# A row-mean kernel: the last store is issued ahead of SyncE's waits for all other transfers

## Chip, cores, metric

One core of one Trainium2 chip. The metric is device microseconds of one launch, median over runs. Kernels that are compared ran in turns in one call on one chip; the three calls of the experiments were on chips 15, 11 and 15.

## Reference

```python
batch, seq, dim = 32, 512, 1024
x = np.random.randn(batch, seq, dim).astype(np.float32)     # 67.1 MB
return (np.sum(x, axis=-1) / divisor).astype(np.float32)    # divisor = 1024.0, 16384 means
```

## The kernel before

The input streams through a few large buffers by transfers that SyncE issues. VectorE sums most rows, ScalarE some. Results leave in three small stores: `res0` (8 KB), `res` (48 KB) and `fin` (8 KB). Only `fin` depends on the last load, `pb`. Engines and transfers report to each other by semaphores, on which the program adds, subtracts and waits (the code below); the landing of the last store shows in the trace as 16 steps of one, from 158.854 to 159.020 us. An event wait (EVENT_SEMAPHORE in the profile) is, in what follows, an instruction of SyncE that only waits: in this trace for one semaphore at 155.914, for two at 157.476. Its passage, below, is the time SyncE takes over it when the counts have long been reached; between two such waits in the changed kernel that is 53 to 64 ns from start to start.

```python
    load(pa, x_last[:, j, :c])
    load(pb[:, : D - c], x_last[:, j, c:])
    tc.keep_in_program_order(nc.sync.dma_start(out=o_first, in_=res0))
    tc.keep_in_program_order(nc.sync.dma_start(out=o_main, in_=res))
    dve_mean(pb[:, D - c : D - c + 1], pa, by=1.0)
    dve_mean(fin[:, j:], pb)
    tc.keep_in_program_order(nc.sync.dma_start(out=o_last, in_=fin))
```

The framework closes a program with a SyncE drain that waits for every transfer and every engine, then two barriers across the engines, with GpSimd clearing semaphores between them. In the trace the waits of SyncE, ScalarE, VectorE and TensorE for the first barrier lie between 158.272 and 158.335, GpSimd's clear (EVENT_SEMAPHORE_RANGE_CLEAR) takes 95 ns from 158.428, and their waits for the second lie between 158.751 and 158.813. This kernel had already been tuned there: a pass over the finished program moves the last store into that closing block, so that its 1.4 us of landing run beside the barriers, and puts the wait for the landing at the very end.

```python
def close_while_storing(nc, landed):
    body, end = nc.main_func.blocks[1], nc.main_func.blocks[-1]
    store = [i for i in body.instructions if i.engine == SP and ...][-1]
    drain = end.instructions[0]
    needs = {w.id: w for w in drain.sync_info.on_wait}
    ...                                   # the store's own transfer is taken off the list
    (done,) = [w for w in store.sync_info.on_wait if w.ant_name.startswith("DVE_")]
    del needs[done.id]                    # VectorE's last result: the store waits for it
    ...                                   # add, sub: +16 and -16 on the semaphore `landed`
    last = nc.sync.wait_ge(landed, 16).ins
    body.instructions = [i for i in body.instructions if i.name != store.name]
    end.instructions = [
        with_sync(drain, on_wait=tuple(needs.values())),        # five event waits and a drain
        with_sync(store, on_wait=(done,), on_update=(add,)),
        *end.instructions[1:-1],                                # the two barriers
        with_sync(last, on_update=(sub,)),                      # the wait for the landing
    ]
```

When the program is built, the drain's list becomes five event waits in front of a drain that keeps one wait; in the trace they start at 155.914 (one semaphore), 156.551, 157.146, 157.310 and 157.476 (two each), and the drain at 157.541.

## Time and profile before

| | before |
|---|---|
| time, median of 3 runs | 160.74 us (160.73 to 160.82) |
| span of the profiled execution | 159.1 us, 147 instructions |
| the DMA queue, share of 16 engines | 98.2% |
| VectorE, ScalarE busy | 117.2 us (74%), 18.5 us (12%) |

The span runs from the first to the last recorded instruction of the kernel; the time of the same execution, 160.59 us, is 1.5 us longer. From the list of transfers, these two rows (line's transfer, issuing queue, count, KB, us from issue to landing) are what SyncE's list waits for last:

```profile
out_dram<-res SPq DMA_DIRECT2D x1, 48.0 KB, 11.6
out_dram<-res SPq DMA_DIRECT2D x1, 8.0 KB, 33.6
```

They are small stores in the queue of the big loads: these 8 KB took 33.6 us to land, the 8 KB of `fin`, issued after the last load has landed, 1.4 us. The 8 KB store of `res0`, issued at 123.7 us, lands at 157.29; the 48 KB store of `res`, issued at 145.9, lands at 157.46: both just in front of VectorE's last result.

### The profile page before, as it was taken

What the parts mean: (1) busy time and instruction counts of PE and PEld (TensorE: products, weight loads), DVE (VectorE), ACT (ScalarE), POOL (GpSimd) and SP (SyncE); (2) the same over time, 40 slices, a digit from 0 to 9 for tenths busy, and PEclk for the clock granted to TensorE, in tenths of its full rate; (3) what the DMA queues carried; (4) which work ended last, traced back from release to release, by engine and by line L of the source; (5) the groups of instructions that cost most, each with busy time, mean ns of one, the idle gap of its engine ahead of it and who ended that gap; (6) DMA issues with size and microseconds to landing.
All of it is one profiled execution on the core that took longest, in us unless ns stands there. A gap on an engine that the chain in (4) does not pass through costs nothing.

```text
span 159.1 us, 147 instructions
## 1 busy us (share of the span) xinstructions
DVE 117.2 (74%) x29; ACT 18.5 (12%) x33; POOL 1.0 (1%) x7
## 2 busy tenths in 40 slices
DVE  0500059995999599977999599959995996395643
ACT  3000000000000000000000000000000900390684
POOL 0000000000000000000000000000000000001000
DMA  8999999979999999789999999699999999999894
GB/s 303 422 461 461 461 461 461 433 317 404 461 461 461 461 461 461 317 375 461 461 461 461 461 461 418 303 433 461 461 461 429 396 396 445 445 445 445 375 406 159
DMA packets 2448, 67.18 MB, mean 422 GB/s; under 512 B 656, under 2 KB 656, under 8 KB 912
## 3 DMA queue, kind: packets, MB, share of 16 engines
q1 hardware_dynamic: 2448, 67.18, 98.2%
HBM read 67.11 MB, written 0.07 MB: 422 GB/s over the span
## 4 chain that ended last, share of the span: by engine, by line
DMA 77%; DVE 21%; SPq 1%; issue 0%; DVEq 0%
DMA t<-in_x_dram 56%; DMA pb<-in_x_dram 21%; DVE res L177 20%; SPq L154 1%; DVE pb L164 0%; DVEq L231 0%
## 5 line engine op out<-in xcount | busy, mean ns | idle before, releaser
L177 DVE TENSOR_REDUCE res<-t 128x14 f32<-128x14336 f32 (+3 forms) x9 | 111.2, 12360 | 34.1 <-DMA t<-in_x_dram 34.1
L158 ACT ACTIVATE junk<-t 128x1024 f32<-128x1024 f32 x16 | 16.2, 1013 | 136.9 <-DMA t<-in_x_dram 136.9
L164 DVE CUSTOM_DVE_ANT_0 t<-t 128x512 f32<-128x512 f32 x8 | 5.1, 690 | 6.1 <-DMA t<-in_x_dram 6.1
L158 ACT ACTIVATION_READ_ACCUMULATOR junk<-t 128x1 f32 x16 | 3.0, 187 | 0.0
L179 POOL TENSOR_SCALAR res<-res 128x16 f32<-128x16 f32 (+1 forms) x2 | 0.7, 352 | 143.3 <-DVE res L177 143.3
L158 ACT ACT_TABLE_LOAD x1 | 1.3, 1283 | 1.7 <-PEq L217 1.7
L164 DVE DVE_READ_ACCUMULATOR2_ANT fin<- 128x1 f32 x9 | 0.8, 83 | 0.0
L164 DVE CUSTOM_DVE_ANT_0 pb<-pb 128x257 f32<-128x257 f32 x1 | 0.4, 428 | 0.2 <-DMA pb<-in_x_dram 0.2
L164 DVE CUSTOM_DVE_ANT_0 pa<-pa 128x256 f32<-128x256 f32 x1 | 0.4, 426 | 0.0
L151 POOL MEMSET pb<- 128x2 f32 x1 | 0.1, 99 | 1.3 <-POOLq L217 1.3
L217 POOL MEMSET const-bfloat16-1.0<- 128x1 bf16 x1 | 0.1, 102 | 0.0
L217 POOL MEMSET const-uint8-127<- 128x1 uint8 x1 | 0.1, 101 | 0.0
L217 POOL MEMSET const-float32-0.0<- 128x1 f32 x1 | 0.1, 98 | 0.2 <-issue 0.2
L217 POOL MEMSET const-float32-1.0<- 128x1 f32 x1 | 0.1, 98 | 0.0
L164 DVE DVE_READ_ACCUMULATOR2_ANT pb<- 128x1 f32 x1 | 0.1, 84 | 0.0
## 6 DMA issues: line engine op xcount, KB each, us to landing
t<-in_x_dram SPq DMA_DIRECT2D x7, 7168.0 KB, 35.6
t<-in_x_dram SPq DMA_DIRECT2D x1, 6144.0 KB, 33.3
t<-in_x_dram SPq DMA_DIRECT2D x1, 4608.0 KB, 27.2
t<-in_x_dram SPq DMA_DIRECT2D x2, 1024.0 KB, 19.2
t<-in_x_dram SPq DMA_DIRECT2D x1, 2048.0 KB, 31.7
pa<-in_x_dram SPq DMA_DIRECT2D x1, 256.0 KB, 33.9
pb<-in_x_dram SPq DMA_DIRECT2D x1, 256.0 KB, 33.9
out_dram<-res SPq DMA_DIRECT2D x1, 48.0 KB, 11.6
```

Of the source, the lines that this page charges most:

```text
L151: nc.gpsimd.memset(pb[:, D - c :], 0.0)
L154: tc.keep_in_program_order(nc.sync.dma_start(out=dst, in_=src))
L158: nc.scalar.activation(junk, src, COPY, scale=by, accum_out=dst)
L164: nc.vector.tensor_tensor_reduce(out=src[:, :h], in0=src[:, :h], in1=src[:, h:], scale=by, scalar=0.0, op0=ADD, op1=ADD, accum_out=dst,)
L177: nc.vector.reduce_sum(out=dst[:, j : j + d], in_=t[:, :d, :], axis=AX)
L179: nc.gpsimd.tensor_scalar_mul(out=dst, in0=dst, scalar1=scale)
L217: nc = _bacc.Bacc("TRN2", target_bir_lowering=False, num_devices=1)
```

## The change

The intent: SyncE should not have to get through its waits for all other transfers before it may issue the last store. Since the store needs only the results in `fin`, it goes first and takes along its own waits; the list comes behind it, still ahead of the barriers.

```diff
     end.instructions = [
+        with_sync(store, on_wait=store.sync_info.on_wait, on_update=(add,)),
         with_sync(drain, on_wait=tuple(needs.values())),
-        with_sync(store, on_wait=(done,), on_update=(add,)),
         *end.instructions[1:-1],
```

In the built program the store gets one event wait in front of it (a load and ScalarE's 16th result) and keeps its wait for VectorE; the five event waits and the drain stand behind it.

## The prediction

0.00 (step 1) + 0.00 (step 2) + 0.10 (step 5) = +0.10 us, hence 160.84 us; the +0.27 us of step 3 and the +0.05 us of step 4 are not added to it but go into step 5. That step took the steps of semaphore 2 for a chain from engine to engine, which was an assumption of mine.

> **What bounds the kernel now.** I read the page of the profiled execution first, then the chain of waits that ended last, then the last two microseconds by timeline and by line, then the time stamps of single instructions and semaphore updates in the trace, because everything the change touches lies in the last 1.5 us of 159.1 us.
>
> The page says what the body of the kernel is: one long load.
>
> ```profile
> DVE 117.2 (74%) x29; ACT 18.5 (12%) x33; POOL 1.0 (1%) x7
> q1 hardware_dynamic: 2448, 67.18, 98.2%
> ```
>
> The one DMA queue fills 98.2% of 16 engines' time with 67.18 MB; no engine is nearly as full. The change leaves all loads and all arithmetic alone, so some 157 of the 159.1 us cannot move. What remains is the end of the chain:
>
> ```profile
> 123.15 0.04 issue
> 123.19 33.94 DMA pb<-in_x_dram
> 157.13 0.02 issue
> 157.15 0.43 DVE pb L164
> 157.58 0.01 DVEq L231
> ```
>
> The last load (pb, issued at 123.19) lands at 157.13, and the last VectorE sum runs 157.15 to 157.58. The reader should note that no wait of SyncE stands between the load and that sum. The timeline shows what follows:
>
> ```profile
> 157.15 0.43 DVE L164 CUSTOM_DVE_ANT_0 pb<-pb 128x257 f32<-128x257 f32 x1 [0.16 <-DMA pb<-in_x_dram]
> 157.50 0.08 DVE L164 DVE_READ_ACCUMULATOR2_ANT fin<- 128x1 f32 x1
> 157.62 0.33 SPq L200 DMA_DIRECT2D out_dram<-fin  x1
> ```
>
> The store of fin starts 0.03 us after the accumulator read ends. The question of the whole case is what those 0.03 us are: the semaphore, or SyncE coming late out of its list of waits. SyncE's list of waits says who it waited for (total us, times, longest):
>
> ```profile
> SPq L231 <- DMA t<-in_x_dram: 9.7, 1, 9.7
> SPq L231 <- DMA pa<-in_x_dram: 0.6, 1, 0.6
> SPq L231 <- PEq L231: 0.6, 2, 0.4
> SPq L231 <- DMA pb<-in_x_dram: 0.6, 1, 0.6
> SPq L87 <- SPq L87: 0.3, 1, 0.3
> ```
>
> and the closing line L231, between 157.2 and 157.56 us, says when its instructions ran:
>
> ```profile
> L231 SPq EVENT_SEMAPHORE  x2: 28/28/28, 157.3 to 157.5; - x2
> L231 SPq DRAIN  x1: 7/7/7, 157.5 to 157.5; - x1
> ```
>
> The waits look large (9.7, 0.6, 0.6 us) but they are over before the store can go. By the stamps, SyncE's last two waits start at 157.310 and 157.476, its drain runs 157.541 to 157.548, VectorE's semaphore reaches its count at 157.598, and the store starts at 157.615. So SyncE was through its list 50 ns before the data existed. The 17 ns from semaphore to start are the same as at the earlier loads that waited for VectorE (121.286 to 121.302, 104.375 to 104.391: 16 ns each). The margin is thin, but the store is already as early as its data allows.
>
> The store's landing and the closing line then run beside each other:
>
> ```profile
> DMA to landing us min/median/max: 1.4/1.4/1.4
> ```
>
> Landing: the store's 16th increment is at 159.020, and the very last wait (the line L87 above, 0.3 us of waiting) ends at 159.053, which is the span. Closing: the store's issue ends at 157.947, SyncE's drain for the barrier runs 157.998 to 158.127, two barriers follow, and SyncE leaves the second at 158.768. The landing path thus beats the closing path by 159.036 - 158.768 = 0.27 us. That slack is what the change spends.
>
> [...] 0.33 us of issue, 1.4 us to landing. [...] a satisfied wait to the next instruction on SyncE, is 65 ns (157.476 to 157.541)[...]. [...] semaphore 2 steps nine times from 159.048 and nine times again from 160.362 to 160.720, which is 8 hops of 45 ns. I use it in step 5.
>
> **The change part by part.** I compared the two built programs. No load, no arithmetic and no other engine's order differ. On SyncE:
>
> 1. Moved: the store from behind five event waits and a drain to ahead of them. Its VectorE wait stays. Gain on the path: the store started 17 ns after its semaphore, so 0.00 us.
> 2. Added: one event wait ahead of the store (the last big load and ScalarE's 16th result). ScalarE's 16th step is at 157.079, the load's landing long before (137.688). It is through by about 157.1, 0.5 us before VectorE's 157.598. Cost 0.
> 3. Shifted: the five event waits and the drain now stand between the store's issue and SyncE's arrival at the first barrier. All they wait for has happened: the latest, the two earlier stores, landed at 157.293 and 157.459. So each costs only its passage. Start: 51 ns after the issue (157.947 to 157.998 now; 124.115 to 124.166 likewise for an event wait after a store). Then 6 x 65 ns = 0.39 us, so the barrier's drain starts at 158.388 in place of 157.998. Given back: that drain takes 129 ns directly behind the store (125 behind the first loads), but 7 ns where no DMA is just ahead; with 0.39 us in between I take 7. It ends at 158.395 in place of 158.127: closing is +0.27 us. Taking 54 ns (17 + 37, a one-semaphore wait and the smallest gap seen) or 89 ns (28 + 61, the gap between two waits on GpSimd) for 65 gives +0.20 to +0.41.
> 4. The end of the span: SyncE leaves the second barrier at 158.768 + 0.27 = 159.04; the store lands at 159.020 as before; the last wait follows 45 ns later (GpSimd's gap from drain to a satisfied wait) and ends near 159.10. Span +0.05 us. The slack has swallowed the rest.
> 5. Behind the span: [...] In the first series the steps are at 159.048, 159.082, 159.287, 159.331 and on; in the second the same steps are 34, 39, 44 ns apart. So the third step came late in the first series, by 205 - 39 ns. The first is 0.235 us after TensorE's sequencer leaves the kernel's last barrier (158.813), the third 0.234 us after SyncE ends (159.053); from that match I take the chain as TensorE first, SyncE third, SyncE late by its wait for the landing. With closing +0.27 the first two steps go to 159.318 and 159.352 and the third to 159.391, while SyncE's own end allows 159.334. The chain, and all that follows it, moves by 159.391 - 159.287 = +0.10 us: not the 0.27 of the closing path, not the 0.05 of the span. The order of the engines is inferred; no view names them.
>
> Sum: 0.00 + 0.00 + 0.10 = +0.10 us on 160.74: 160.84 us, or +0.06%.
>
> **Rivals.**
> (a) The intended gain: the store goes earlier and the end with it. For it: only 50 ns of margin, so in an execution where the two small stores land later than VectorE's last sum, SyncE would be late in the kernel before. Against: in the traced one the store went 17 ns after its semaphore; even removing all of the 28 ns after VectorE ends gives nothing like a per cent. It would make 160.65 to 160.74.
> (b) The closing path becomes the bound and costs in full: if the waits pass slowly[...]. Against: the 65 ns seen.
> (c) Full cover: the waits pass in 54 ns and the chain after the span hangs on the landing alone: 160.74 to 160.77.
> (d) Loads move: none. The store is 8 KB and goes after the last load has landed, so it can delay nothing.
>
> **Range and chances.** [...]the three runs of before spread over 0.09 us (160.73 to 160.82) and its profiled run took 160.59, so a run or a chip differs by as much as the effect. I put the middle at 160.84 and 8 in 10 at 160.6 to 161.1. 2% would be 3.2 us; nothing in the last 1.5 us can move that much, save a state I cannot see. Same 0.98, faster 0.01, slower 0.01.
>
> **What would show it.** In the changed profile the store's issue should again start about 17 ns after VectorE's last semaphore (step 1), with an event wait of SyncE near 157.1 ahead of it (2), five waits and a drain about 65 ns apart behind it, and a barrier drain of 7 ns (3); the wait for the landing should shrink from 0.3 us to under 0.1, and the span grow by 0.0 to 0.2 (4). I am wrong if the store starts earlier against its semaphore, if the barrier's drain still takes 0.13 us, [...]or if the time falls by more than the spread of the runs.

## The result and the profile after

The changed kernel took 161.01 us (median of 6 runs, 160.91 to 161.35), the kernel before 160.75 in the same rounds (160.63 to 160.82). The ratio is 1.002, interval 1.0007 to 1.0033. By the 2% mark that is the same; by the interval it is a small loss. A ratio here is the mean time of one kernel's fast runs over that of the other's of the same rounds, so it is not quite the ratio of the medians quoted.

The timeline of the last two microseconds, changed kernel (start, duration, engine, line):

```profile
157.36 0.43 DVE L165 CUSTOM_DVE_ANT_0 pb<-pb 128x257 f32<-128x257 f32 x1 [0.16 <-DMA pb<-in_x_dram]
157.71 0.08 DVE L165 DVE_READ_ACCUMULATOR2_ANT fin<- 128x1 f32 x1
157.82 0.33 SPq L201 DMA_DIRECT2D out_dram<-fin  x1
```

The store again follows the last accumulator read by 0.03 us: nothing was gained there. The whole group sits 0.2 us later than before because in this execution the last load landed at 157.33, not 157.13. So it is better to count from VectorE's last semaphore (157.598 before, 157.804 after) than from the start of the span.

SyncE's waits in the changed kernel (who waited, for whom, total us, times, longest):

```profile
SPq L201 <- ACT junk L159: 11.1, 1, 11.1
SPq L232 <- PEq L232: 0.6, 2, 0.4
SPq L201 <- DVE fin L165: 0.5, 1, 0.5
```

The waits at the closing line for the loads of t, pa and pb are gone from the list, and so is the last line of before, 0.3 us at line L87. That one was SyncE sitting at the end of the program until the store had landed. After the change the store has been down for 0.05 us when that last wait runs.

Where SyncE spent that time instead shows at the closing line between the store's issue and the first barrier. Before, from 157.95 to 158.15:

```profile
L231 SPq DRAIN  x1: 129/129/129, 158.0 to 158.0; - x1
```

After, from 158.15 to 158.59:

```profile
L232 SPq EVENT_SEMAPHORE  x5: 17/28/28, 158.2 to 158.4; - x5
L232 SPq DRAIN  x2: 7/7/7, 158.5 to 158.6; - x2
```

(Durations are ns: least, median, most; then first and last start.) One drain of 129 ns became five event waits, the drain of the list and the barrier's drain, now 7 ns. By the stamps the event waits start 53, 62, 64 and 61 ns apart, the list's drain 65 ns and the barrier's drain 59 ns later.

The remaining evidence is in single stamps, which no view lists; the table below gives them as us after VectorE's last semaphore. "Chain" is my name for the steps of semaphore 2 behind the kernel, which no instruction of the kernel touches. In before they are nine from 159.048 to 159.572 us and nine more from 160.362 to 160.720; between 159.475 and 160.138 the trace has a last update of 247 semaphores, numbers 7 to 255. The expectations call it the runtime's chain; whose it is, no trace shows. The time of an execution is the last step of that chain, counted from the start of the span, less 0.11 to 0.13 us in all fourteen traces: in before 160.72 and 160.59, in after 161.16 and 161.04, in the kernel tail30 below 161.38 and 161.26. So the last step stands for the metric.

| kernel | store starts | SyncE at the first barrier | TensorE ends | SyncE ends | chain: step 1 | step 2 | step 3 | step 5 | last step |
|---|---|---|---|---|---|---|---|---|---|
| before | 0.017 | 0.529 | 1.215 | 1.455 | 1.450 | 1.484 | 1.689 | 1.756 | 3.122 |
| after | 0.016 | 0.766 | 1.451 | 1.484 | 1.686 | 1.720 | 1.925 | 1.993 | 3.356 |
| difference | 0.00 | +0.24 | +0.24 | +0.03 | +0.24 | +0.24 | +0.24 | +0.24 | +0.23 |

SyncE's own end hardly moved, as predicted. The chain moved nevertheless, by all of the 0.24 us that SyncE lost on its way to the barrier.

### The profile page after: what moved, and what is told of

The parts are those of the page before. It is cut to its first block, busy times and chain, and to the rows that moved or that the text cites. A ratio compares the mean times of both kernels' runs of the same rounds, so it can differ in the third digit from the quotient of the medians.

```text
span 159.3 us, 148 instructions
## 1 busy us (share of the span) xinstructions
DVE 117.2 (74%) x29; ACT 18.5 (12%) x33; POOL 1.0 (1%) x7
## 4 chain that ended last, share of the span: by engine, by line
DMA 77%; DVE 21%; SPq 1%; issue 0%; DVEq 0%
DMA t<-in_x_dram 56%; DMA pb<-in_x_dram 21%; DVE res L178 20%; SPq L155 1%; DVE pb L165 0%; DVEq L232 0%
```

## The experiments

Theory A: what counts is when the kernel's two closing barriers are through; the chain starts from there, so each passage that stands between the store and SyncE's first barrier is paid in full. Theory B, which my prediction rested on: SyncE's wait for the landing holds the chain at its third step, so part of the loss is hidden. Theory C: the change also makes the loads end later, since the first trace had them 0.2 us later.

All kernels gave correct results. "Chain" is the last step after VectorE's last semaphore; before has 3.122 in its first trace and 3.129 in the second.

### Controls: the changed kernel twice more, the kernel before against itself

No edit (`after_again`, `after_last`, `before_again`).

> The changed kernel once more, unedited. Theory A (the whole closing path is paid: SyncE reaches its first barrier 0.24 us later against VectorE's last semaphore[...]): time +0.24 us over before, and the last load lands as in before, so the 0.2 us by which the loads ended later in its first trace were chance. Theory B (my prediction's step 5: SyncE's wait for the landing holds the runtime's chain at its third step, so part is hidden): +0.10 us. Theory C (the change also makes the last loads land 0.2 us later): +0.4 us and pb landing again near 157.33.

> The kernel before against itself: ratio 1.000, the interval shows what a run can tell (about 0.1% = 0.15 us). A and B: pb lands anywhere from 157.1 to 157.4 us; C: always near 157.13. In all: SyncE's barrier drain ends 0.53 us after VectorE's last semaphore, the third step of the runtime's chain 1.69 us after it.

> The changed kernel a third time, in the third place of its call: the +0.3 us of means so far is over the 0.24 us that the closing path shows in each trace. Theory A: the rest is when the loads end, which varies alike in both kernels: ratio 1.0015 (+0.24 us), trace again 0.24 us later from VectorE's last semaphore to the end. Theory C (loads made later by the change too): ratio 1.002 or more again with pb landing later than in the other traces of this call.

| run | median | ratio to before, 95% | pb lands | chain |
|---|---|---|---|---|
| after_again | 161.15 us, 6 runs | 1.0020 (1.0004 to 1.0036) | 157.152 | 3.360 |
| after_last | 161.02 us, 5 runs | 1.0019 (0.9999 to 1.0038) | 157.541 | 3.356 |
| before_again | 160.67 us, 6 runs | 0.9991 (0.9977 to 1.0005) | 157.238 | 3.129 |

Counted from VectorE's last semaphore, the last step of three executions of the changed kernel agrees to 4 ns, that of two of before to 7 ns. There the difference is 0.23 to 0.24 us, as A has it. The loads are another matter. In after_again pb landed as early as in before, against C; in after_last it was the latest, which is what C expected. In that trace the delay was there by 123.51 us, where one of the large loads lands (123.08 to 123.31 in the other traces), over 20 us ahead of the point at 146.3 us where SyncE's two programs first differ. In the first trace of the changed kernel, though, it first shows at the load that lands at 148.74, behind that point. With means of +0.31 to +0.33 us and 0.24 explained, some 0.1 us stays open (taken up again at the end of the next section).

### Extra waits behind the landing

```diff
+    more = [nc.sync.wait_ge(landed, 16).ins for _ in range(6)]      # tail30: range(30)
     last = nc.sync.wait_ge(landed, 16).ins
...
-        *end.instructions[1:-1],
+        *end.instructions[1 : -1 - len(more)],
+        *more,
         with_sync(last, on_update=(sub,)),
```

The edit was made on the kernel before. The build packs two waits into one event wait: 30 waits are 15 in the profile below, and tail6 has three instructions more than before (150 against 147).

> The kernel before with 3 more event waits (already satisfied, 62 ns each) at the very end of SyncE, behind the wait for the landing: SyncE ends 0.19 us later, both closing barriers as before. B: third step of the runtime's chain 0.19 us later and time +0.19 us. A: the third step stays 1.69 us after VectorE's last semaphore, time +0.0 us.

> The same with 15 more event waits: SyncE ends 0.93 us later. B: time +0.93 us. A: SyncE is the holder only from some lateness on; the runtime's chain shows at which step SyncE stands and how much slack it had: the time grows by 0.93 us less that slack, which tail6 puts at 0.19 or more.

| run | median | ratio to before, 95% | SyncE ends | step 3 | step 4 | step 5 | last step |
|---|---|---|---|---|---|---|---|
| before | | | 1.455 | 1.689 | 1.733 | 1.756 | 3.122 |
| tail6 | 160.75 us | 0.9995 (0.9981 to 1.0009) | 1.636 | 1.691 | 1.735 | 1.765 | 3.124 |
| tail30 | 161.35 us | 1.0034 (1.0021 to 1.0047) | 2.371 | 1.690 | 1.734 | 2.507 | 3.820 |

In tail30 the extra waits stand in one line of the profile, running from 159.0 to 159.8 us, well behind the barriers:

```profile
L87 SPq EVENT_SEMAPHORE  x15: 17/28/28, 159.0 to 159.8; - x15
```

This refutes B. Step 3 does not move though SyncE ends 0.92 us later; steps 2 and 3 are 205 ns apart in before and in after alike, and step 3 stays at 1.69 in tail6 and tail30. Step 5 is the one that goes with SyncE: it comes 0.136 us after SyncE's end in tail30 (2.371 to 2.507) and 0.13 in tail6. In before it could have ended 1.756 - 0.136 - 1.455 = 0.165 us later without moving step 5. To the last step it had 0.22 us to spare: tail30's end is 0.916 us later and its last step 0.698, because step 6 follows step 5 by 44 ns there, against 97 in before. tail6 shows the slack: its span is 0.3 us longer (159.4 against 159.1), of which 0.18 come from SyncE's end and the rest from the loads, but counted from VectorE's last semaphore its last step is where it was (3.124 against 3.122), and the median is unchanged. A span that grows at SyncE's end and a time that grows are two things.

### Half of the change; one wait; a drain replaced

Half of the change, `half_behind`: three entries ahead of the store, two event waits and the drain behind it.

```diff
-        with_sync(drain, on_wait=tuple(needs.values())),
+        with_sync(ready, on_wait=ahead, on_update=()),
         with_sync(store, on_wait=(done,), on_update=(add,)),
+        with_sync(drain, on_wait=behind),
...                                   # cut: ready, and how ahead and behind are picked from needs
```

> Half of the change: two event waits and the drain behind the store, the other waits ahead. Theory A (each passage behind the store is paid in full): the two passages take 53 and 62 ns, so SyncE's barrier drain should start 0.05 + 0.05 + 0.06 + 0.06 us after the store's issue and end at 0.58 us after VectorE's last semaphore in place of 0.53: time +0.05 us. Theory B (the landing hides it): 0.00. Too small for the time alone; the trace decides by the first step of the runtime's chain, 1.45 us after VectorE's last semaphore in before: A 1.50, B 1.50 as well but fifth step unmoved at 1.76 against A 1.81.

One satisfied event wait behind the store, the list ahead as before, `one_behind`:

```diff
         with_sync(store, on_wait=(done,), on_update=(add,)),
+        with_sync(extra, on_wait=(done,), on_update=()),
...                                   # cut: extra, an event wait
```

> The kernel before with one satisfied event wait between the store and SyncE's barrier drain. If the 129 ns of that drain are owed only directly behind a DMA instruction, the wait (53 ns) replaces them by 7 and closing is 0.07 us EARLIER: barrier drain ends 0.455 us after VectorE's last semaphore instead of 0.53, time -0.07 us. If the drain waits for a fixed end of the DMA's work, it still ends at 0.53 and time is 0.00. If each instruction just adds, 0.58 and +0.05 us.

The barrier's first drain replaced, `fused_arrival`, run twice:

```diff
+    sync = rest[at].sync_info          # rest[at]: SyncE's drain at the first barrier
+    rest[at] = with_sync(arrive, on_wait=sync.on_wait, on_update=sync.on_update)
...                                   # cut: rest is the two barriers, put back in their place
```

where `arrive` is an event wait.

> The kernel before with SyncE's drain at the first barrier replaced by an event wait that signals the same semaphores. Under A, SyncE signals 0.41 us after VectorE's last semaphore instead of 0.53: the chain and the time 0.12 us shorter (160.62 from 160.74), with SyncE's wait for the landing then 0.05 us from being the holder (its slack was 0.17 us by the tail runs). Under B (the landing holds): 0.00 us.

> The best version so far once more: its chain ended 0.11 us earlier against VectorE's last semaphore, its time was 0.9996 of before with an interval across 1. Expected -0.11 us (ratio 0.9993); the interval will hardly leave 1.

| run | median | ratio to before, 95% | store starts | SyncE at the first barrier | step 1 | last step |
|---|---|---|---|---|---|---|
| half_behind | 160.78 us | 1.0003 (0.9991 to 1.0015) | 0.017 | 0.585 | 1.507 | 3.177 |
| one_behind | 160.80 us | 1.0001 (0.9989 to 1.0013) | 0.017 | 0.528 | 1.449 | 3.120 |
| fused_arrival | 160.59 us | 0.9996 (0.9983 to 1.0008) | 0.024 | 0.419 | 1.339 | 3.008 |
| fused_again | 160.65 us | 0.9994 (0.9977 to 1.0011) | 0.070 | 0.465 | 1.385 | 3.056 |

No time here is told from before by its interval; the traces are. Every change of SyncE's arrival comes out at the last step one for one: +0.056 gives +0.055, 0.00 gives 0.00, -0.110 gives -0.114, -0.064 gives -0.066. Step 5 of half_behind moved as A said (1.813), not as B.

one_behind settles the drain. Its line, in the stretch 158.2 to 158.35 us:

```profile
L233 SPq DRAIN  x1: 83/83/83, 158.2 to 158.2; - x1
```

With the 53 ns of a wait in front of it the drain took 83 ns, not 129, and ended at 0.528, where it ended before (0.529). So the second of the three expectations held: in both traces the drain ends 0.51 us after the store's start. Two other traces agree: a drain of SyncE that begins 0.461 us after the store's start takes 51 ns in arrive_first (below), and one that begins 0.499 us after it takes 14 ns in half_behind; both end at 0.51. (The figure is this store's: in before the drain behind the third load, with an issue of 0.43 us in place of 0.33, ends 0.61 us after that load's start.) Up to there the wait of one_behind was free behind the store; the change put 0.36 us of passages there, of which 0.12 us took the place of the drain's.

fused_again was a miss by half, and for a reason of its own: the store started 53 ns late. In that execution the 48 KB store landed at 157.552, only 71 ns ahead of VectorE's last semaphore, and SyncE was not through the list when the data was ready. This is the loss that the change was meant to remove. It exists in some executions, but against the 0.24 us that the change costs it is small: 9 ns in before_again, 7 in fused_arrival, 53 in fused_again.

### The opposite order: arrive first, then store

```diff
-        with_sync(store, on_wait=(done,), on_update=(add,)),
-        *end.instructions[1:-1],
+        with_sync(ready, on_wait=(done,), on_update=()),  # an event wait
+        *rest[: at + 1],                                  # SyncE signals the first barrier
+        with_sync(store, on_wait=(), on_update=(add,)),
+        *rest[at + 1 :],
```

> The opposite of the change: SyncE waits for VectorE, signals the first barrier, and only then issues the store. The barriers end about 0.3 us earlier, the store about 0.11 us later. If the closing path alone set the time: -0.3 us. With the landing as the other gate (SyncE is the fifth step of the runtime's chain, 0.13 us after its end, slack 0.17 us in before): fifth step at 1.70 us after VectorE's last semaphore instead of 1.76, time -0.05 us. B as predicted (landing is the gate already): +0.11 us.

Measured: 160.67 us, ratio 0.9998 (0.9985 to 1.0011). The store starts at 0.150 and SyncE ends at 1.581, but TensorE ends at 0.871 and the chain's first step is at 1.105, 0.345 earlier than before. The last step is at 3.030, a gain of 0.09 us. In SyncE's list of waits the one for the landing is now long:

```profile
SPq L88 <- SPq L88: 0.8, 1, 0.8
```

Here the landing is the gate, at step 5 (1.721, which is 0.140 after SyncE's end), and 0.25 us of the 0.345 are lost to it. Closing and landing are two paths to one chain; before, closing was the longer, by 0.22 us at the last step, and here landing is.

### A case in which the list really ends late

Both orders, with the store of `res0` issued behind that of `res` and held back until VectorE's last sum but one:

```diff
+    early = [i for i in body.instructions if i.engine == SP and ...][-1]
+    held = dataclasses.replace(done, wait_value=done.wait_value - 1)
+    ...                # held is added to the waits of early, the store of res0
-    tc.keep_in_program_order(nc.sync.dma_start(out=o_first, in_=res0))
     tc.keep_in_program_order(nc.sync.dma_start(out=o_main, in_=res))
+    tc.keep_in_program_order(nc.sync.dma_start(out=o_first, in_=res0))
```

> A case in which the list of waits really ends late: the 8 KB store of res0 is held back until VectorE's last sum but one (0.60 us before its last semaphore), so that it lands 1.40 us after its issue, some 0.83 us behind VectorE's last semaphore. Order of before. Theory A: the wait for that landing now stands in front of the last store, which starts near 0.97 us after VectorE's last semaphore in place of 0.02; chain and time +0.96 us.

> The same held-back store in the order of the change. Theory A: the last store starts at 0.02 us again, and only the closing waits for the landing: SyncE's barrier drain ends near 0.97 us in place of 0.53, time +0.45 us on before, so 0.5 us FASTER than late_store_before: here the change pays. If the order of store and waits did not matter beyond the passages: both the same.

| run | median | ratio to before, 95% | store of fin starts | SyncE at the first barrier | last step |
|---|---|---|---|---|---|
| late_store_before | 161.67 us | 1.0061 (1.0040 to 1.0081) | 1.021 | 1.535 | 4.128 |
| late_store_after | 161.08 us | 1.0019 (1.0004 to 1.0035) | 0.017 | 1.028 | 3.623 |

From SyncE's list of waits in the order of before, the wait for the held-back store:

```profile
SPq L237 <- DMA out_dram<-res: 0.8, 1, 0.8
```

and from the timeline of the same kernel, VectorE's last result and the store of it:

```profile
157.52 0.08 DVE L170 DVE_READ_ACCUMULATOR2_ANT fin<- 128x1 f32 x1
158.64 0.33 SPq L206 DMA_DIRECT2D out_dram<-fin  x1
```

In the order of the change, SyncE's list of waits has

```profile
SPq L238 <- DMA out_dram<-res: 0.3, 1, 0.3
```

and the timeline

```profile
157.68 0.08 DVE L171 DVE_READ_ACCUMULATOR2_ANT fin<- 128x1 f32 x1
157.78 0.33 SPq L207 DMA_DIRECT2D out_dram<-fin  x1
```

In the order of before the wait for the held-back store stands in front of the last one, and 1.03 us pass between the end of the accumulator read and the store. In the order of the change that wait overlaps the issue of the last store. The change gains 0.505 us in the chain and 0.6 in the medians; against the 2% mark this is small too, but the two intervals do not overlap. Both kernels came out some 0.05 us later than expected, because the held store started 0.03 to 0.04 us later than I had put it and landed 1.42 and 1.41 us after its start, not 1.40. The change is sound, then; the kernel it was put on had next to nothing for it to remove.

## Why the prediction was right, and where its working was not

The measured 161.01 us lie in the range (160.6 to 161.1), and "same" was right. The sign was right: no gain at the store, a small loss behind it. The size of the loss was not: +0.10 us predicted, +0.24 in the traces, +0.26 between the medians. That the range held is partly luck: it was laid around the wrong middle, 160.84, and another median of the same kernel, 161.15 in after_again, lies outside it.

1. The store starts no earlier: right. 17 ns after VectorE's semaphore before, 16 or 17 after. The margin, though, was misread: the 50 ns from the end of the list's drain to the semaphore leave out the passage from that drain to the store. Where SyncE was late (before_again, fused_arrival, fused_again), the store starts 59 ns after that drain's start. In before the drain started at 157.541, so the store could have gone at 157.600, only 15 ns before it did.
2. The added wait in front of the store costs nothing: right. It was through at 157.308, 0.5 us before the store could go. But it does not appear where I looked for it, near 157.1: the profile has it as one instruction from 146.28, 11.03 us long (ScalarE's 16th step came at 157.286).
3. The closing path becomes 0.27 us longer: it became 0.237. The gap behind the store was 47 ns for 51 and the six passages took 53 to 65 ns for the 65 assumed. The drain's 7 ns were right, and one_behind shows why: behind this store the drain ended at 0.51 us with a wait in front of it and without, and here it starts 0.74 us after the store.
4. SyncE's end moves by 0.05 us: it moved by 0.03. Near enough, and without meaning for the time.
5. "from that match I take the chain as TensorE first, SyncE third, SyncE late by its wait for the landing": this step failed. TensorE's end does lead step 1 by 0.235 us in before, after and tail30, so the chain starts from the closing barriers. But SyncE is step 5, not 3, and the 0.234 us from its end to step 3 were a coincidence of before: in after it is 1.925 - 1.484 = 0.44. I had taken the landing to hold the chain, so that the closing path could grow by 0.17 us for nothing. It was the other way round: the closing path held the chain and the landing had the slack, so nothing of the 0.237 us was hidden. The term of the sum is +0.24, not +0.10.

Rival (b), that the closing path is paid in full, is thus what happened, at 0.24 us, with the short passages of 53 to 65 ns. Rival (a), an earlier store, is real, at 0.01 to 0.05 us in single executions. Rival (c), full cover, was refuted by the same shift. Rival (d), that no load moves, is what stays open:

The changed kernel's 17 timed runs have a mean of 161.10 us; before's 37 runs (the six of before_again left out) have 160.77. Of the 0.33 us, 0.24 are the closing path. The traces put VectorE's last semaphore at 157.80, 157.62 and 158.01 in the changed kernel, against 157.60 and 157.71 in before and 157.56 to 157.80 in the nine edited kernels' traces. In the first of the three the load that lands at 148.74 takes 11.06 us from the landing before it, 10.85 to 10.89 in the others. Three traces cannot tell 0.1 us of such spread from a cause, and each ratio's interval includes 1.0015. By the spread of the single runs (0.21 and 0.18 us) the difference of the two means has a standard error of 0.06 us, so the open 0.1 us is 1.7 of these. I take it for chance, which is not shown.

A version better than both is fused_arrival by its two traces, 0.07 and 0.11 us ahead of before at the last step; its timed ratios of 0.9996 and 0.9994 have intervals that include 1, so in time this is not shown either.

## What to carry to other kernels

The wait in front of the store cost nothing where it ended before the store's own, in the changed kernel (157.308 against 157.804); where it ended later, in late_store_before, the store started 1.0 us later. So look up when each of the waits ended before moving anything, because the totals in a list of waits (9.7 us here) do not say it. The waits moved off the path to the store landed on the path to the first barrier (+0.24 us): find which of the paths at the end of a program is the longer one, and by how much, before counting slack. Where the span and the time part, as in tail6 against after, an experiment that delays only one engine's end shows which engines the time hangs on.
